# Hyena filters and DFT operands as f16 pairs, conditioning inside the first filter spectrum, row squares between the filter's steps

## The chip, the cores and the metric

One core of a Trainium2 chip runs the whole program as one launch. The metric is the device time of an execution in microseconds, as the median of several runs; lower is better.

## The reference

Two layers of a diffusion backbone: 1024 latent tokens and 256 context tokens of 1024 channels. The first layer mixes half of its channels by a 2-D Fourier transform and half by an order-2 Hyena operator, the second by neighbourhood attention; each ends with a SwiGLU. The norms are modulated by vectors that a matrix product of a conditioning vector gives (`ada_mod`). The change concerns the Hyena filters, the first norm and its modulation:

```python
def ada_mod(cond, w, b):
    m = (jax.nn.silu(cond) @ w + b)[..., None, :]
    return jnp.split(m, 6, axis=-1)

def hyena_filters(L, w1, b1, freq, w2, b2, w3):
    ...
    h = jnp.sin(freq * (z @ w1 + b1))
    h = jnp.sin(freq * (h @ w2 + b2))
    h = (h @ w3).reshape(L, 2, HY_ORDER, HY_CH)
    ...
    h = h * jnp.exp(-t01 * deltas)[:, None, None, :]
    h = h / jnp.sum(jnp.abs(h), axis=(0, 1), keepdims=True)
    fwd, bwd = h[:, 0], h[:, 1]
    return jnp.concatenate([fwd, jnp.zeros_like(fwd[:1]), bwd[:0:-1]], axis=0)

def long_conv(u, filt, skip):
    ...
    ff = jnp.fft.rfft(filt, n=2 * L, axis=0)
    y = jnp.fft.irfft(uf * ff[None], n=2 * L, axis=1)[:, :L]
    return y + u * skip
```

For each token `u = rms_norm(x, g) * (1 + scale) + shift` follows, and `p = u @ w_in` is the first large product. There are filters for length 1024 (latent, called `l`) and for length 256 (context, `c`), two orders each.

## The kernel before, in words

The program is written as Python generators that issue instructions in steps and are woven into each other in `run`. A scheduler then fixes the order of each engine's instructions before the launch; on the chip every engine issues its own in that order. Tiles come from pools with a number of buffers by tag: `p4` (`S4`, 20 of 4 KB a partition), `p2` (`S2`, 34 of 2 KB), `pt` and `pk` (`T`, `TK`), `pw` (three tags `ws`, `wh`, `wl` with two buffers each), eight PSUM banks (`ps`, `pq`). DMAs go by the SP queue (`ld`) or by the POOL queue (`ldr`, also for loads that cast).

Ahead of the input projection stand these steps.

- `filter_mlp`: two small fp32 layers with a sine behind each, for 512 latent and 128 context positions, in both directions. Its output is split for PE into a high part and a remainder, stacked on the partitions (`ta`, `tb`).
- `ada_first`: the shift and scale of the first norm. Sixteen loads `ada_k` of 512 KB, in eight steps of two, each step with four fp32 products of two columns (L423) into one PSUM bank; then four copies of its rows to SBUF (L431), sixteen small fp32 products that turn them into columns, and additions. `operand_scale` makes of them one factor, with a maximum over partitions on POOL (L1238), by which `norm_half` forms its f16 pairs.
- `filter_raw`: `w3` of the two directions is added and subtracted (L626), split into fp32r pairs (`split`: a cast on ACT, L287, and a subtraction on DVE, L289), multiplied with `ta` and `tb` and by a window (L646). For each order, 4 blocks with a forward and a backward half, even and odd.
- `filter_spectrum`: four DFT matrices (`ff`) by four blocks. For each of the sixteen pairs, an operand is formed on DVE (L707 to L713), split into an fp32r pair (L287, L289), and multiplied with the matrix, which comes as f16 high and low halves and is cast to fp32r on ACT (`cmat`, L335): three products for each of four outputs. `filter_sum` runs within: absolute values on ACT (L658, L659), a maximum and a running sum on DVE (L660, L662), a sum over partitions on PE.
- `norms` in `run`: ten row tiles of x are squared with an accumulator on ACT (L2149), a square root and reciprocal follow, then the reciprocals are spread over partitions by fp32 products of a diagonal with ones (L2158 to L2162), then 24 calls of `norm_half`, two passes on DVE and one on ACT each (L555 to L558).

In `run` before, `ada_first` is stepped from the start through `filter_raw` of the first order and drained ahead of the first spectrum. The raw values of the second order, and four `norm_half`, go into the first spectrum, the other twenty into the second. The context filter is filler work of `in_proj`, whose sixteen weight blocks follow; there its w3 sums (L626) and its operands are on POOL.

## Time and profile before

| What | Value |
|---|---|
| Runs | 2910.8, 2916.38, 2915.75 us, median 2915.75 |
| Profiled execution | 2919.95 us; its span 2918.2 us, mean TensorE clock 0.977 |
| Busy over the span | PE 2766.6, DVE 2094.0, ACT 1647.7, POOL 642.6 us |
| First product of the first spectrum | 69.67 us from the span's start |
| Last product of the second spectrum ends | about 198.2 us |
| First product of the input projection | 205.69 us |
| `ada_k` loads | 16 of 512 KB, median 6.2 us from issue to landing |
| `x_row` loads | 10 of 512 KB, median 9.8 us |

Times of a row are microseconds from the start of the span; a row of a group has its busy time, the mean of one instruction in ns, and the idle time of the engine just before. The busy time of TensorE takes in the time at a reduced clock, so the granted clock is read beside it.

### The profile page before, as it was taken

How to read it: one execution, taken by the hardware profiler on the slowest of the kernel's cores; microseconds unless marked ns; L12 is line 12 of the kernel's file. 1: busy time of each engine (PE TensorE's matmuls, PEld its weight loads, DVE VectorE, ACT ScalarE, POOL GpSimd, SP SyncE). 2: the span in 40 equal slices, each digit the busy share in tenths (PEclk: the TensorE clock that was granted, in tenths of full speed). 3: DMA queues.
4: the chain of work that ended last, by engine and by line, in shares of the span. 5: the costliest groups of instructions: out<-in, count | busy, mean ns of one | idle time of the engine just before them, and what ended most of it. 6: DMA issues, size and time to landing. Idle time of an engine off the chain costs nothing. (4 is left out here: it accounts for less than half of the span.)

```text
span 2918.2 us, 46050 instructions
## 1 busy us (share of the span) xinstructions
PE 2766.6 (95%) x16163; PEld 1714.2 (59%) x16163; DVE 2094.0 (72%) x3833; ACT 1647.7 (56%) x2899; POOL 642.6 (22%) x1057
## 2 busy tenths in 40 slices
PE   6989999999989999999999999999999999999998
PEld 3766557888879644444555844676665444444554
DVE  4778867585467798877886767776676778775765
ACT  4674324454675667654555555676664477654553
POOL 1012013354220121213120012444443022112000
PEclk8989999999999999999999999999999999999999
DMA  6574434358785555566994798777775666424753
GB/s 254 187 265 161 161 122 151 111 168 286 285 344 182 207 205 197 201 213 240 327 333 161 273 337 294 179 188 172 185 198 188 236 226 231 153 93 184 242 191 113
DMA packets 325156, 615.98 MB, mean 211 GB/s; under 512 B 90934, under 2 KB 130552, under 8 KB 324922
## 3 DMA queue, kind: packets, MB, share of 16 engines
q1 hardware_dynamic: 252378, 384.38, 39.9%
q0 software_dynamic: 70240, 224.45, 21.6%
q10 hardware_dynamic: 2304, 4.20, 0.4%
q8 instruction: 127, 2.08, 0.3%
q14 instruction: 107, 0.88, 0.1%
HBM read 455.33 MB, written 135.53 MB: 202 GB/s over the span
## 5 line engine op out<-in xcount | busy, mean ns | idle before, releaser
L1449 PE MATMUL ps<-s,s 128*128 128x512 f16 x2592 | 582.2, 382 | 14.4 <-ACT tk L1454 6.8
L1449 PEld LDWEIGHTS <-s 128*128 128x128 f16 x2640 | 259.0, 98 | 332.6 <-issue 27.8
L283 PE MATMUL ps<-s,wh 128*128 128x256 f32 (+3 forms) x1752 | 398.2, 331 | 11.1 <-ACT wh L287 5.4
L1218 ACT ACTIVATE s<-s,c 128x512 f16<-128x512 f32 (+1 forms) x324 | 233.5, 754 | 141.9 <-DMA s<-d 79.9
L1219 DVE SCALAR_TENSOR_TENSOR s<-s,c,s 128x512 f16<-128x512 f32 (+1 forms) x324 | 247.4, 794 | 84.5 <-ACT s L1218 84.1
L1666 PE MATMUL ps<-s 128*128 128x512 f16 (+2 forms) x1308 | 303.4, 378 | 2.0 <-DVE s L1219 2.0
L283 PE MATMUL pq<-s,wh 128*128 128x512 f16 (+1 forms) x1000 | 280.3, 354 | 9.8 <-DMA wh<-d 5.4
L283 PE MATMUL ps<-s,wl 128*128 128x256 f32 (+3 forms) x876 | 261.6, 331 | 1.3 <-DVE wl L289 1.2
L283 PEld LDWEIGHTS <-wh 128*128 128x128 f16 x1664 | 160.9, 99 | 170.2 <-issue 20.9
L1666 PEld LDWEIGHTS <-s 128*128 128x128 f16 x1536 | 148.5, 98 | 178.9 <-issue 6.5
L274 POOL DMA_DIRECT2D d<-s x201 | 109.0, 543 | 640.5 <-DVE s L1510 178.6
L283 PE MATMUL ps<-s,s 128*128 128x65 f16 (+5 forms) x2666 | 222.3, 236 | 27.5 <-DMA s<-s 11.4
L335 ACT CAST mat<-cs 128x1024 fp32r<-128x1024 f16 (+2 forms) x120 | 111.6, 935 | 140.6 <-PE ps L283 57.3
L283 PEld LDWEIGHTS ps<-s,wh 128*128 128x128 f32 x1088 | 177.5, 192 | 18.1 <-ACT wh L287 5.7
L283 PE MATMUL ps<-s,mat 128*128 128x512 f32 x696 | 184.7, 413 | 3.3 <-DVE s L289 2.9
L1449 PE MATMUL ps<-s,wh 128*128 128x512 f16 x616 | 184.9, 379 | 1.8 <-DVE g L1463 1.4
L283 PE MATMUL pq<-s,wl 128*128 128x512 f16 (+1 forms) x500 | 174.5, 354 | 0.5 <-DMA wl<-d 0.5
L283 PEld LDWEIGHTS <-s 128*128 128x128 f16 x2400 | 114.5, 98 | 82.9 <-DMA s<-s 11.5
L283 PEld LDWEIGHTS ps<-s,mat 128*128 128x128 f32 x696 | 136.5, 199 | 37.9 <-DVE s L289 3.8
L1251 ACT ACTIVATE t<-s 128x1024 bf16<-128x1024 f32 (+1 forms) x164 | 141.9, 867 | 12.2 <-DVE c L470 8.4
L283 PEld LDWEIGHTS ps<-s,s 128*128 128x128 f32 (+1 forms) x746 | 113.6, 192 | 32.1 <-ACT s L287 7.0
L283 PEld LDWEIGHTS <-wl 128*128 128x128 f16 x832 | 82.3, 99 | 77.4 <-issue 4.5
(431 smaller groups left out, 5477.3 us busy)
## 6 DMA issues: line engine op xcount, KB each, us to landing
s<-d SPq DMA_DIRECT2D x294, 256.0 KB, 4.0
d<-s POOLq DMA_DIRECT2D x157, 256.0 KB, 3.2
s<-in_down SPq DMA_DIRECT2D x154, 256.0 KB, 5.4
s<-in_ada_w POOLq DMA_DIRECT2D x48, 512.0 KB, 4.8
g<-in_bias POOLq DMA_DIRECT2D x128, 192.0 KB, 3.6
s<-in_gate SPq DMA_DIRECT2D x46, 512.0 KB, 3.7
s<-in_up SPq DMA_DIRECT2D x46, 512.0 KB, 4.0
d<-g POOLq DMA_DIRECT2D x87, 256.0 KB, 2.9
```

What stands on the lines that cost most here:

```text
L274: self.last_ldr = self.nc.gpsimd.dma_start(out, in_).ins
L283: self.nc.tensor.matmul(o, l, r, start=st, stop=sp)
L335: self.nc.scalar.copy(m, st)
L1218: nc.scalar.activation(hi, src, AF.Copy, scale=scale)
L1219: nc.vector.scalar_tensor_tensor(lo, src, scale, hi, op0=MUL, op1=SUB)
L1251: self.nc.scalar.activation(junk[:, :t.shape[1]], t, AF.Abs, scale=2.0 ** -15, accum_out=st[:, k:k + 1])
L1449: nc.tensor.matmul(ps, x[:, sl], y, start=first and j == 0 and x is wh and y is xh, stop=j == 3 and x is wl, skip_group_check=True)
L1666: m = nc.tensor.matmul(acc[j][:, c0:c1], x[:, sl], y[:, xs], start=first and k == 0, stop=last and k == 2, skip_group_check=True)
```

## The change

Eight edits, all in the part ahead of the input projection and in the context filter.

1. `ta`, `tb`, the pairs of w3, of the DFT operands and of the first row become f16 instead of fp32r. The matrices are used as they come, in f16, in three buffers; their cast on ACT goes.
2. The w3 of an order is divided by one factor: absolute values on ACT, sums over partitions by two bf16 products, a maximum along the row, times 2^-14.
3. The context filter loads the pairs of w3 that the latent filter has stored in DRAM instead of forming them on POOL, ACT and DVE.
4. `ada_first` is stepped in the first eight steps of the first spectrum, drained in the ninth with `operand_scale`; its loads go to `S4` buffers.
5. The squares of the rows are issued one a step between the steps of `filter_raw` and the first spectrum, no longer held behind the split of w3; three window tiles are loaded early, ahead of the rows.
6. `filter_mlp` yields twice a layer, so that the steps of w3 can come between.
7. The running sum of `filter_sum` goes from DVE to POOL.
8. In the second order, the operands of even blocks go from DVE to POOL (except those with a mask).

The constant `PAD_C` goes from 176 to 160. The core of the diff:

```diff
     def ada_first(self):
...
-            ws = [self.mat(1024, F32) for _ in range(2)]
+            ws = [self.S4() for _ in range(2)]
...
+    def split16(self, src):
+
+        t = self.S2(F16, 1024)
+        self.nc.scalar.copy(t[:, :512], src)
+        self.nc.vector.tensor_tensor(t[:, 512:], src, t[:, :512], SUB)
+        return t[:, :512], t[:, 512:]
...
     def filter_raw(self, sq, raws, os=(0, 1)):
...
+                ab = self.T(BF16, 1024)
+                ps = sums[o] = self.PS()
+                for j in (0, 1):
+                    nc.scalar.activation(ab[:, j * 512:j * 512 + 512], st[(o, j)], AF.Abs)
+                for j in (0, 1):
+                    self.mm(ps, self.ones.bitcast(BF16)[:, 1::2], ab[:, j * 512:j * 512 + 512], j == 0, j == 1)
+            yield
+            ts, big = {}, self.C(2)
+            for o in os:
+                nc.vector.tensor_reduce(big[:, 0:1], sums[o], axis=AX, op=MAX)
+                nc.vector.tensor_scalar(big[:, 1:2], big[:, 0:1], 1e-30, 2.0 ** -14, op0=MAX, op1=MUL)
+                nc.vector.reciprocal(big[:, 0:1], big[:, 1:2])
...
+                x = self.S2(F16, 1024)
+                self.half_split(t, big[:, 0:1], x[:, :512], x[:, 512:])
+                self.ldr(self.w3d[key], x)
...
     def filter_sum(self, sq, o, raw):
...
-                    nc.vector.tensor_tensor(acc, acc, t, ADD)
+                    nc.gpsimd.tensor_tensor(acc, acc, t, ADD)
...
     def filter_spectrum(self, sq, o, raw):
...
-                        (nc.vector if sq == "l" else nc.gpsimd).tensor_tensor(t, f, r, ADD if i in (0, 3) else SUB)
-                    xh, xl = self.S2(F32R), self.S2(F32R)
-                    self.split(t, xh, xl)
-                    yield xh, xl, self.cmat(2 * nb * P, a["ff_" + sq][i, b])
+                        eng = nc.vector if sq == "l" and (o == 0 or b % 2) else nc.gpsimd
+                        eng.tensor_tensor(t, f, r, ADD if i in (0, 3) else SUB)
+                    xh, xl = self.split16(t)
+                    mt = self.mat16(2 * nb * P)
+                    self.ld(mt, a["ff_" + sq][i, b])
+                    yield xh, xl, mt
...
     def run(self):
...
-        for _ in range(4):
-            next(ada1)
         with self.tc.issue_after(self.clamp), self.tc.issue_after(self.sin):
             next(fr)
-        for i, _ in enumerate(fr):
-            next(ada1, None)
-            if i in (0, 4):
-                next(ng)
-        drain(ada1)
-        self.u0col, self.usi = self.operand_scale(0, 0, (0, 1))
+        for _ in fr:
+            next(ng)
         fr = self.filter_raw("l", raws["l"], (1,))
         for i, _ in enumerate(self.filter_spectrum("l", 0, raws["l"][0])):
+            if i < 8:
+                next(ada1)
+            elif i == 8:
+                drain(ada1)
+                self.u0col, self.usi = self.operand_scale(0, 0, (0, 1))
             if i >= 2:
                 next(fr, None)
-            if i >= 11:
+            if i < 5 or i >= 11:
                 next(ng)
```

What the scheduler makes of it shows at three places. The first is ACT at the start. Before, it ran both sines of the filter's layers, the casts for the first raw products (`s_52`, `s_53` from the second sine, `s_71` from the sum of w3), and then the squares:

```order
L592 ACTIVATE s_44_142<-s_44_142 128x640
L592 ACTIVATE s_48_157<-s_48_157 128x640
L599 CAST s_52_172<-s_48_157 64x512
L601 CAST s_53_173<-s_48_157 64x512
L599 CAST s_54_178<-s_48_157 64x128
L601 CAST s_55_179<-s_48_157 64x128
L287 CAST s_71_225<-t_223 128x512
L287 CAST s_74_231<-t_229 128x512
L2149 ACTIVATE s_34_122,c_265<-s_34_122 128x1024
L2149 ACTIVATE s_35_124,c_265<-s_35_124 128x1024
```

Now five squares (the last one is shown) stand ahead of the first sine, and these rows follow:

```order
L2194 ACTIVATE s_41_136,c_240<-s_41_136 128x1024
L598 ACTIVATE s_47_148<-s_47_148 128x640
L2194 ACTIVATE s_42_138,c_240<-s_42_138 128x1024
L2194 ACTIVATE s_43_140,c_240<-s_43_140 128x1024
L2194 ACTIVATE s_44_142,c_240<-s_44_142 128x1024
L2194 ACTIVATE s_45_144,c_240<-s_45_144 128x1024
L2194 ACTIVATE s_46_146,c_240<-s_46_146 128x1024
L2196 ACT_TABLE_LOAD
L2196 ACTIVATE c_240<-c_240,c_95 128x10
L598 ACT_TABLE_LOAD
L598 ACTIVATE s_57_177<-s_57_177 128x640
L607 CAST s_61_192<-s_57_177 64x512
```

The squares, their square root and two table loads moved from behind the second sine to ahead of it. The second place is PE. Before, the last conditioning products (`mat` is a tile of `ada_k`, `c_115` the conditioning vector) were followed by the columns' products (`c_86`), the spread of the norms' reciprocals (`c_91`), and only then, eight rows on, by the first DFT product:

```order
L423 MATMUL ps_190<-mat_328,c_115 2x512 x2
L423 MATMUL ps_190<-mat_329,c_115 2x512 x2
L283 MATMUL ps_346<-c_86,g_347 128x2 x4
L283 MATMUL ps_346<-c_86,g_353 128x2 x4
L283 MATMUL ps_363<-c_86,g_364 128x2 x4
L283 MATMUL ps_363<-c_86,g_370 128x2 x4
L283 MATMUL ps_381<-t_378,c_91 128x256
L283 MATMUL ps_390<-tk_385,c_91 128x512
L283 MATMUL ps_399<-tk_394,c_91 128x512
```

Now the first conditioning products stand behind the first four DFT products (`m_117` is a matrix, `s_116` the high and low half of an operand):

```order
L283 LDWEIGHTS m_117_326
L283 MATMUL ps_331<-s_116_323,m_117_326 128x512
L427 MATMUL ps_353<-s_126_354,c_115 2x512 x2
L427 MATMUL ps_353<-s_127_355,c_115 2x512 x2
L427 MATMUL ps_353<-s_131_384,c_115 2x512 x2
L427 MATMUL ps_353<-s_132_385,c_115 2x512 x2
L427 MATMUL ps_353<-s_136_414,c_115 2x512 x2
L283 LDWEIGHTS c_206
L283 MATMUL pq_319<-s_116_323,c_206 2x512
```

The other eleven tiles of `ada_k` are spread over the rows up to the end of the third matrix. The third place is DVE in the fourth matrix of the first spectrum, where the scale of the conditioning (`c_754`) is formed. Its first row waits for POOL's maximum over partitions (L1284, formerly L1238); on POOL that stands behind the three running sums of L705. Before, the same rows stood ahead of the whole spectrum.

```order
L1285 TENSOR_SCALAR c_754<-c_754 128x1
L1286 RECIPROCAL c_754<-c_754 128x1
L689 TENSOR_TENSOR s_271_891<-ps_929,s_284_927 128x512
L1290 TENSOR_SCALAR c_754<-c_101,c_754 128x16
L1290 TENSOR_SCALAR c_754<-c_102,c_754 128x16
L559 SCALAR_TENSOR_TENSOR t_940<-s_274_898,c_754,s_176_541 128x256
L758 TENSOR_TENSOR t_944<-s_99_274 128x512
L559 SCALAR_TENSOR_TENSOR t_979<-s_274_898,c_754,s_176_541 128x256
```

An operand of that spectrum (`t_944`, L758) is now formed behind the scale and the first norm passes (L559).

More of the change, by code (lines that the diff above doesn't have):

```diff
@@ L593, in filter_mlp @@
             x = s
+            if layer == 0:
+                yield
         self.tap("mlp", x)
@@ L610, in filter_mlp @@
         self.frg, self.rn, self.kap = {}, {}, {}
+        self.w3d = {(o, eo): self.DR([P, 1024], F16) for o in (0, 1) for eo in (0, 1)}
+    def split16(self, src):
[3 more added lines that the diff above has]
+        return t[:, :512], t[:, 512:]
     def filter_raw(self, sq, raws, os=(0, 1)):
@@ L615, in filter_raw @@
         nb = 4 if sq == "l" else 1
[L616 to L629 removed]
+        w3, win = {}, {}
@@ new lines, in filter_raw @@
+        if sq == "c":
+            for key, d in self.w3d.items():
+                t = self.S2(F16, 1024)
+                self.ld(t, d)
+                w3[key] = (t[:, :512], t[:, 512:])
+        else:
+            st = {}
+            for o in os:
+                for j in (0, 1):
+                    st[(o, j)] = self.S2()
+                    self.ld(st[(o, j)], a["w3"][:, (2 * j + o) * HC:(2 * j + o + 1) * HC])
+            for b, k in ((0, 0), (0, 1), (1, 0)):
+                win[(b, k)] = self.S2()
+                self.ld(win[(b, k)], a["win_l"][b, k])
+            yield
+            sums = {}
+            for o in os:
+                ab = self.T(BF16, 1024)
+                ps = sums[o] = self.PS()
+                for j in (0, 1):
+                    nc.scalar.activation(ab[:, j * 512:j * 512 + 512], st[(o, j)], AF.Abs)
+                for j in (0, 1):
+                    self.mm(ps, self.ones.bitcast(BF16)[:, 1::2], ab[:, j * 512:j * 512 + 512], j == 0, j == 1)
+            yield
+            ts, big = {}, self.C(2)
+            for o in os:
+                nc.vector.tensor_reduce(big[:, 0:1], sums[o], axis=AX, op=MAX)
+                nc.vector.tensor_scalar(big[:, 1:2], big[:, 0:1], 1e-30, 2.0 ** -14, op0=MAX, op1=MUL)
+                nc.vector.reciprocal(big[:, 0:1], big[:, 1:2])
+                for eo, op in ((0, ADD), (1, SUB)):
+                    t = ts[(o, eo)] = self.T()
+                    nc.vector.tensor_tensor(t, st[(o, 0)], st[(o, 1)], op)
+            yield
+            for key, t in ts.items():
+                x = self.S2(F16, 1024)
+                self.half_split(t, big[:, 0:1], x[:, :512], x[:, 512:])
+                self.ldr(self.w3d[key], x)
+                w3[key] = (x[:, :512], x[:, 512:])
@@ L2146, in norms @@
             sq = self.C(10)
-            with self.follow(self.last_hi):
-                for i, t in rows:
-                    nc.scalar.activation(t, t, AF.Square, accum_out=sq[:, i:i + 1])
+            for i, t in rows:
+                nc.scalar.activation(t, t, AF.Square, accum_out=sq[:, i:i + 1])
+                yield
             nc.scalar.activation(sq, sq, AF.Sqrt, scale=1.0 / D, bias=self.eps)
```

44 lines of the change are left out of this document (21 added, 23 removed).

## The prediction

> **What bounds the kernel now.** I began with the stages (busy time by window), because the change touches only the first 206 us and, thinly, the filler work of the input projection behind them.
>
> ```profile
> 0.00:69.67 69.67, 41.06 (x143) 19.74 (x144) 28.55 (x64) 30.13 (x56) 11.19 (x27) 0.80 0.73 266
> 69.67:198.20 128.53, 118.30 (x484) 92.16 (x483) 100.28 (x161) 90.61 (x133) 1.28 (x2) 0.92 0.58 193
> 198.20:205.70 7.50, 0.17 (x2) 0.01 (x1) 0.64 (x5) 7.50 (x15) 0.00 (x0) 0.71 1.04 401
> ...
> 205.70:480.00 274.30, 263.51 (x1430) 154.76 (x1431) 210.88 (x432) 99.66 (x175) 46.61 (x53) 0.96 0.44 156
> ```
>
> The columns are window, length, busy PE, PEld, DVE, ACT, POOL, the granted TensorE clock, the DMA share and GB/s. In the first 69.67 us PE is busy 41. From 69.67 to 198.2 (the two filter spectra) it is busy 118.3 of 128.5 at a mean clock of 0.92, so 10.2 us are idle and about 8% (10.3 us) go to the slow clock. From 198.2 to 205.7 PE has nothing and ACT is full. From 205.7 on PE is the bound. Next I read what PE waited for before 206.
>
> ```profile
> PE ps L283 <- ACT s L287: 9.1, 3, 5.9
> ...
> PE ps L283 <- DVE s L289: 2.9, 2, 2.7
> ...
> PE ps L283 <- DVE s L662: 2.6, 1, 2.6
> ```
>
> The columns are the wait in all, the times, the longest. 5.9 of the first row lie before the first raw product; the other 3.2 of it, 2.9 and 2.6 are gaps inside the spectra. Then the timeline, for when the first spectrum could start and what stood ahead of it.
>
> ```profile
> 24.05 0.74 ACT L592 ACTIVATE s<-s 128x640 f32<-128x640 f32 x1 [7.56 <-DVE s L591]
> ...
> 27.42 0.79 PE L283 MATMUL ps<-s,s 128*128 128x512 f32 x1 [5.86 <-ACT s L287]
> ...
> 33.88 0.69 DVE L646 TENSOR_TENSOR s<-ps,s 128x512 f32<-128x512 f32 x1 [5.05 <-DMA s<-in_win_l]
> ...
> 44.72 1.29 DVE L713 TENSOR_TENSOR t<-s 128x512 f32<-128x512 f32 x2
> ...
> 52.37 3.08 PE L423 MATMUL ps<-mat,c 128*2 128x512 f32 x8 [2.91 <-DMA mat<-in_ada_k]
> ...
> 55.49 2.38 ACT L431 COPY g<-ps 2x512 f32<-2x512 f32 x4 [4.94 <-PE ps L423]
> ...
> 56.21 6.96 PE L283 MATMUL ps<-c,g 2*128 2x2 f32 x32 [0.77 <-ACT g L431]
> ...
> 69.67 0.84 PE L283 MATMUL ps<-s,mat 128*128 128x512 f32 x3
> ```
>
> DVE has formed the first operands by 46 (44.72 + 1.29), yet the first product with a DFT matrix (`mat`) runs at 69.67. Between them lies the conditioning: 8 MB of `ada_k` through two pairs of buffers, its products (L423), four copies on ACT (L431), the turn into columns. ACT issues in order, so the cast of the first operand stands behind copies that wait for PE. **This chain, not work, sets 69.67.**
>
> **The change, part by part.** The times are of the profiled execution, 2919.95 us with its span of 2918.2; the median of the runs is 2915.75, so 4.2 less.
>
> *A. The front without the conditioning.* The new ACT order puts five squares ahead of the first sine and five, with a square root and two table loads, between the two.
>
> ```profile
> 15.75 0.74 ACT L592 ACTIVATE s<-s 128x640 f32<-128x640 f32 x1 [4.36 <-DVE s L591]
> ...
> L2149 ACT ACTIVATE s<-s 128x1024 f32<-128x1024 f32 x10 | 10.4, 1046 | 0.0
> ...
> L2150 ACT ACT_TABLE_LOAD x1 | 1.3, 1283 | 0.0
> ...
> 35.68 3.07 DVE L646 TENSOR_TENSOR s<-ps,s 128x512 f32<-128x512 f32 x5
> ```
>
> The first sine was at 15.75; DVE now does two sums and the maximum of the w3 sums ahead of it (three 0.68 passes and three small ones), from which I subtract a little because 2 MB of `ada_k` no longer stand ahead of the w3 loads: 17.5 (bounds 15.75 and 20). The second follows at 17.5 + 0.7 + five squares at 1.04 + two table loads at 1.28 + 0.3 = 26.3; by the MLP alone it would be 24.05 - 15.75 = 8.3 after the first, 25.8. As before, 3.3 us later the first raw product: 29.6. It runs eight high halves before the first low one (at the slow clock about 0.4 each), so the first multiplication by the window is at 32.7; the window tiles are loaded ahead of the rows now, and the 5.05 wait goes. DVE then has 16 of them at 0.61 (the row with x5) and 4.3 us of others in front of the first operand: 46.5. One cast, 0.6: **47.1 instead of 69.67, 22.6 earlier** (bounds: 26, with the sine 1.75 earlier and DVE not held by the raw products; 16, with it 2.5 later and 4 lost to rows of x that land late). PE's 32 raw products fit beneath DVE here.
>
> *B. What moves into the first spectrum.*
>
> ```profile
> L423 PE MATMUL ps<-mat,c 128*2 128x512 f32 x64 | 13.4, 721 | 5.0 <-DMA mat<-in_ada_k 5.0
> ...
> L283 PE MATMUL ps<-c,g 2*128 2x2 f32 x32 | 7.0, 348 | 0.8 <-ACT g L431 0.8
> ...
> L283 PE MATMUL ps<-tk,c 128*128 128x512 f32 x4 | 3.6, 1061 | 0.0
> ...
> L283 PE MATMUL ps<-t,c 128*128 128x256 f32 x2 | 1.2, 715 | 0.0
> ...
> 50.00:60.00 10.00, 6.87 (x26) 4.01 (x27) 0.21 (x3) 4.75 (x7) 0.00 (x0) 0.56 0.28 89
> 60.00:70.00 10.00, 9.49 (x28) 6.58 (x29) 3.01 (x18) 3.19 (x7) 0.38 (x1) 0.59 0.34 100
> ```
>
> 13.4 of L423 at the mean clock 0.80-0.85 are 11.4 at full clock; 7.0 + 3.6 + 1.2 lay at 56 to 68, at a clock of 0.56 to 0.59, so 6.8. Sum 18.2, plus 0.5 for the w3 sums; bounds 15 and the measured 25.2. PE was the busy engine there, so all of it counts. Its 16 loads are issued by POOL behind two writes of w3 halves, which wait for DVE at about 31; 47 leaves time for the first six, and the later ones come in pairs between products.
>
> *C. Half precision.* The two sorts of 512-column product at full clock:
>
> ```profile
> 117.83 2.93 PE L283 MATMUL ps<-s,mat 128*128 128x512 f32 x12
> ...
> 120.59 0.62 PE L283 MATMUL pq<-s,s 128*128 128x512 f32 x2
> ...
> 187.85 1.84 PE L283 MATMUL ps<-c,s 128*128 128x1 f32 x16
> ...
> 211.82 0.27 PE L283 MATMUL pq<-s,wh 128*128 128x256 f16 x1
> 211.93 0.59 PE L283 MATMUL ps<-s,wh 128*128 128x512 f16 x2
> 212.36 0.27 PE L283 MATMUL pq<-s,wh 128*128 128x256 f16 x1
> ```
>
> Twelve fp32r in 120.59 - 117.83 = 2.76, 0.230 each; 1280 columns of f16 in 0.54, 0.216 per 512. By the code there are 384 with `mat`, 36 small ones for the first row, 32 raw ones of the second order: 452 x 0.014 = **6.3**. The lighter weights (fp32r loads take 0.19, f16 0.10) lie beneath the products.
>
> *D. Casts and waits.*
>
> ```profile
> L335 ACT CAST mat<-cs 128x1024 fp32r<-128x1024 f16 x32 | 33.4, 1051 | 34.0 <-issue 12.4 <-PE ps L283 10.4 <-PE ps L423 5.2
> ...
> L662 DVE TENSOR_TENSOR s<-s,s 128x1024 f32<-128x1024 f32 x6 | 7.3, 1211 | 0.0
> ...
> L713 POOL TENSOR_TENSOR t<-s,s 128x512 f32<-128x512 f32 x2 | 2.5, 1274 | 0.0
> ...
> 86.92 0.80 PE L283 MATMUL pq<-s,s 128*128 128x512 f32 x1 [1.98 <-ACT s L287]
> ...
> 88.03 4.81 PE L283 MATMUL ps<-s,mat 128*128 128x512 f32 x12
> ```
>
> 32 casts, 33.4 us, leave ACT, which had 90.6 of 128.5 there: this removes the 1.98 wait, and little else, since ACT ended few of PE's waits. Walking the new order by these durations I find idle PE at three places: 1.7 at the conditioning rows (four accumulator copies of 0.5 and one of 0.6 on ACT, less one conditioning product); 3.4 where the remainder of the fourth matrix's third block stands on DVE behind the scale from POOL's all-reduce and seven operations of 0.4 to 0.6; 3.3 at the start of the second spectrum (four copies and two casts, as before). That is 8.4 against 10.2. An idle time of 2 us costs more than itself: behind the one at 86.92 twelve products take 0.40 each. I keep the loss by the clock at 10.3, as fewer gaps stand against a cold start at 47.1.
>
> The Trainium skill, "TensorE: Matmul & The Clock Gate", section "What's actually happening", says that the clock halves after an idle window and returns after about 3.4 us of work. The trace has 4.8 us and more behind a gap of 2.0, so by the rule three gaps would cost about 5 and not 10.3, and the sum would be 5 lower.
>
> In the second spectrum DVE could become the bound: 32 norm passes of 512 at 0.67, 5 of 256 at 0.4, 14 remainders and 8 operands at 0.6, 4 maxima at 1.13 and small ones, 42 us by the new order, against 210 products at 0.216, 47 with the column sums (1.84 above). It fits, narrowly.
>
> *Sum.* Work after the first product: 128.5 - 10.2 - 10.3 = 108.0, less 6.3, plus 18.7, is 120.4; plus 8.4 idle and 10.3 clock: 139.1. From 47.1 the spectra end at 186.2 (before 198.2). The tail to the first projection product (table load, Silu, copies, weights' sums) keeps its 7.5: 193.7 against 205.7, **12.0 us gained**. Behind that I take nothing: the context filter loses w3 sums on POOL, 8 splits and small casts, but PE is full; bounds 0 and 5. Its one long wait is this:
>
> ```profile
> PE ps L283 <- DVE c L1316: 3.8, 1, 3.8
> ```
>
> 2919.95 - 12.0 = 2908.0 for an execution like the profiled one, and 2915.75 - 12.0 = **2903.8**, called 2904.
>
> **The rivals.** *The conditioning and PE take it all back*: either f16 products come no faster (minus 6.3), or the moved 25.2 cost their measured length (minus 6.5). Gain 5.5 to 6, or nothing with both: 2910 to 2916. Against it: the slow clock of 56 to 68.
>
> *More than forecast*: the removed casts let the operands run so far ahead that only the second spectrum's start stays idle and the clock holds (plus 5 and 5), and the projection's 3.8 wait goes: 18 to 26, 2890 to 2898. For it: ACT and DVE each lose work; against: the in-order remainders behind the conditioning scale.
>
> *Slower: POOL holds DVE.* Six 1024-wide sums and four operands go to POOL.
>
> ```profile
> 208.13 1.21 DVE L470 CUSTOM_DVE_ANT_0 t<-s,s 128x1024 bf16<-128x1024 f32 x1
> ...
> 214.39 2.28 DVE L470 CUSTOM_DVE_ANT_0 t<-s,s 128x1024 bf16<-128x1024 f32 x1
> ...
> 208.66 6.92 POOL L626 TENSOR_TENSOR t<-s,s 128x512 f32<-128x512 f32 x4 [24.87 <-DMA s<-in_w]
> ```
>
> While POOL adds (1.73 each, 1.27 elsewhere), the same DVE operation takes 2.28 and not 1.21. Ten operations, the wide ones doubled to 3.5, are 28 us of POOL; DVE loses about half of that, 14, against 7.3 + 2.7 saved. If it loses all of it, and the all-reduce stands behind three sums of 3.5, PE waits 10.5 more in the first spectrum, 2.4 by the clock, and 6 in the second: 19 lost, 7 slower, 2923. It decides from the point at which DVE's 42 us exceed PE's 47, or the all-reduce ends later than PE's arrival by more than 12.
>
> The Trainium skill, "SBUF — State Buffer", section "SBUF: two separate sides", calls the port pair of DVE and GpSimd an exclusive lock under which the loser blocks fully, for DVE operations with two SBUF inputs. The rows agree in kind (2.28 for 1.21); by full blocking this rival's 2923 holds.
>
> **How the numbers follow.** Forecast (gain 7 to 18, 2898 to 2909): 0.52. More: 0.20. Taken back: 0.17. Slower: 0.11. The range leaves out the slower case and the far end of the larger gain: 2893 to 2915. About 0.2% (5.8 us, 2909.9 and 2921.6) is what a measurement can tell from no change. Faster: 0.52 + 0.20 and a little of the third, 0.74; same 0.16; slower 0.10.
>
> **What would show it.** A: the first product with a matrix (`m`) at 43 to 52. B: the conditioning products between those of the first spectrum, with no DMA wait over 2 us. C: 0.216 between f16 products. D: three gaps as named, PE idle about 8 in the spectra. End: the first projection product near 194. I am wrong if that product comes at 194 and the whole doesn't follow, if DVE's two-input operations double for long stretches, or if the second sine waits for the rows past 30.

## The result and the profile after

The changed kernel takes 2924.92 us (median of 15 runs, 2917.42 to 2928.78) against 2913.04 for the kernel before in the same comparison: ratio 1.0031, 95% interval 1.002 to 1.0043. Two more comparisons gave 1.0023 (1.0008 to 1.0037) and 1.0025 (1.0012 to 1.0037). By these ratios it is slower by 7 to 9 us; 12 faster were forecast, and the forecast is wrong.

The windows of the changed kernel, cut where PE starts the first spectrum, the second, ends it, starts the projection, the long convolution (first L913 product), ends its inverse transform (last L1019) and starts the first feed-forward product (L1495):

```profile
0.00:50.55 50.55, 16.06 (x43) 6.24 (x43) 30.57 (x56) 22.60 (x38) 9.75 (x24) 0.96 0.94 351
50.55:140.14 89.59, 79.42 (x362) 31.02 (x362) 50.10 (x94) 35.71 (x67) 12.04 (x11) 0.91 0.44 152
140.14:198.70 58.56, 51.52 (x226) 21.70 (x226) 52.38 (x71) 35.34 (x57) 23.64 (x9) 0.94 0.62 205
198.70:207.29 8.59, 0.36 (x3) 0.01 (x1) 0.63 (x5) 8.39 (x16) 0.00 (x0) 0.80 0.95 368
207.29:455.00 247.71, 242.95 (x1354) 136.69 (x1355) 194.21 (x407) 83.51 (x147) 37.88 (x47) 0.98 0.47 163
455.00:696.50 241.50, 228.14 (x1448) 204.50 (x1446) 164.49 (x340) 121.00 (x191) 104.38 (x115) 0.97 0.55 172
696.50:983.80 287.30, 267.08 (x1747) 241.49 (x1748) 170.53 (x254) 167.41 (x274) 51.91 (x96) 0.96 0.70 260
```

The front ends 19 us earlier than in the execution shown of before (50.55 for 69.44), and all of it is gone by 207.29. Between them PE's idle time has grown; the gaps on its timeline (two shorter ones, of 0.7 to 0.8, are left out):

```profile
50.55 0.59 PE L283 MATMUL pq<-s,c 128*2 128x512 f16 x1 [7.64 <-ACT s L624]
...
128.64 0.58 PE L283 MATMUL pq<-s,m 128*128 128x512 f16 x1 [5.26 <-ACT s L624]
...
132.10 1.01 PE L283 MATMUL pq<-s,m 128*128 128x512 f16 x2 [1.60 <-DVE s L625]
...
140.14 0.38 PE L283 MATMUL pq<-s,c 128*2 128x512 f16 x1 [1.84 <-ACT s L624]
...
160.71 0.81 PE L283 MATMUL pq<-s,m 128*128 128x512 f16 x3 [2.44 <-ACT s L796]
162.68 1.23 PE L283 MATMUL ps<-s,m 128*128 128x512 f16 x3 [1.17 <-ACT s L624]
...
166.72 2.72 PE L283 MATMUL ps<-s,m 128*128 128x512 f16 x6 [2.39 <-DVE s L625]
...
179.77 0.59 PE L283 MATMUL pq<-s,m 128*128 128x512 f16 x2 [1.04 <-DVE s L625]
...
207.29 2.31 PE L283 MATMUL ps<-s,wh 128*128 128x256 f16 x6 [1.94 <-ACT wh L1264]
```

Behind 50.55 the idle time in the spectra is 17.2 (89.59 - 79.42, and 58.56 - 51.52); 8.4 was forecast. The largest gap, 5.26, hangs on the conditioning: PE waits for the cast on ACT (L624) of an operand that DVE forms behind the scale. POOL's rows and DVE's, in order of time:

```profile
98.69 2.35 POOL L705 TENSOR_TENSOR s<-s,s 128x1024 f32<-128x1024 f32 x1 [12.68 <-DVE s L703]
113.45 2.35 POOL L705 TENSOR_TENSOR s<-s,s 128x1024 f32<-128x1024 f32 x1 [12.42 <-DVE c L1278]
117.02 2.35 POOL L705 TENSOR_TENSOR s<-s,s 128x1024 f32<-128x1024 f32 x1 [1.23 <-DVE s L703]
125.17 0.38 POOL L1284 PARTITION_ALL_REDUCE c<-c  x1 [5.80 <-issue]
```

```profile
112.08 1.22 DVE L703 TENSOR_TENSOR s<-s,s 128x1024 f32<-128x1024 f32 x1
...
113.84 3.04 DVE L703 TENSOR_TENSOR s<-s,s 128x1024 f32<-128x1024 f32 x1
...
117.40 2.05 DVE L1280 SCALAR_TENSOR_TENSOR c<-c 128x1 f32<-128x1 f32 x2
...
120.58 0.14 DVE L1283 TENSOR_TENSOR c<-c 128x1 f32<-128x1 f32 x1
125.58 0.15 DVE L1285 TENSOR_SCALAR c<-c 128x1 f32<-128x1 f32 x1 [4.86 <-POOL c L1284]
```

The all-reduce has its operand at 120.72, and POOL has been free since 119.37, yet it runs at 125.17: 5.80 us of "issue", in which the profile shows nothing that POOL waits for (5.67 and 5.78 in the two other traces of this kernel). DVE stands at the row behind it (L1285) for 4.86, with the operands and remainders that PE needs queued behind. Of the all-reduce (L1284) the view by line has a row on POOL's sequencer:

```profile
L1284 POOLq MODIFY_POOL_CONFIG  x6: 8/11/37, 119.3 to 1259.3; - x6
```

It comes at 119.3, when the last sum is done. I read the 5.8 us as a change of POOL from sums to the all-reduce; the runs without those sums bear it out below. The same view of the kernel before shows such waits too:

```profile
L1238 POOLq MODIFY_POOL_CONFIG  x6: 8/37/37, 47.4 to 1255.7; - x6
L1238 POOL PARTITION_ALL_REDUCE c<-c x4: 378/380/777, 64.2 to 1479.3; - x4
...
  issue: 11.8, 2
```

Two later all-reduces waited 5.9 each on average for "issue"; the first had its change at 47.4 and its operand only at 64, so the change was hidden under the conditioning. The Trainium skill, "GPSIMD Engine Reference", section "2.1 Instruction dispatch", says that the first call of a freshly loaded kernel pays some 6 us (5.95) with no instruction to be seen for it. 5.80 agrees in size, behind a MODIFY_POOL_CONFIG row as there; what POOL does in that time no trace here shows.

**Is the execution shown of before a fair base?** A second trace of the kernel before has these windows:

```profile
0.00:65.74 65.74, 39.08 (x142) 19.23 (x142) 28.54 (x63) 29.88 (x56) 11.19 (x27) 0.84 0.76 281
65.74:134.61 68.87, 62.26 (x258) 48.55 (x258) 51.15 (x86) 43.85 (x64) 0.00 (x0) 0.93 0.52 174
134.61:192.17 57.56, 53.16 (x226) 40.78 (x227) 49.45 (x77) 47.27 (x70) 1.28 (x2) 0.97 0.68 224
192.17:199.85 7.68, 0.17 (x3) 0.01 (x1) 0.63 (x5) 7.68 (x15) 0.00 (x0) 0.85 1.01 358
...
696.80:974.10 277.30, 263.43 (x1747) 239.72 (x1746) 170.69 (x253) 167.15 (x274) 52.12 (x96) 0.97 0.73 268
```

Its first projection product is at 199.85, not 205.69; a third execution with that front (below) has 200.63. The one I forecast from had a late front. Three traces of the changed kernel have 207.29, 210.30 and 209.94. By means (202.1 and 209.2) the change **loses 7.1 us by the first projection product**, and not the 1.6 that the two first traces show.

The lengths of the two spectra vary far less than where they start. From the first product of each to the first of the next, and to the end of the last one (198.90 in the first trace of the changed kernel, so 58.76 and not the 58.56 of the window above):

| Kernel | First spectrum | Second spectrum |
|---|---|---|
| before, three traces | 71.30, 68.87, 70.69 | 57.43, 57.56, 59.02 |
| changed, three traces | 89.59, 89.98, 90.01 | 58.76, 58.74, 58.73 |
| changed, POOL's part undone (e3, e12) | 85.12, 83.85 | 55.95, 56.44 |
| changed, first three sums on DVE (e6) | 83.86 | 60.12 |
| conditioning in front, POOL's part kept (e4) | 64.95 | 59.43 |
| conditioning in front, POOL's part undone (e5) | 65.71 | 56.06 |

Within the changed kernel, idle time and slow clock trade places: its other two traces have gaps of 2.86 and 2.96 where the first has 5.26, and 12.1 and 14.8 idle in all for 17.2, at a mean clock of 0.88 for 0.91 in the first spectrum. The length is the same, so I go by the lengths.

### The profile page after: what moved, and what is told of

Read it like the earlier page. It is cut to its first block, busy times and chain, and to the rows that moved or that the text cites. A ratio compares the mean times of both kernels' runs of the same rounds, so it can differ in the third digit from the quotient of the medians.

```text
span 2918.1 us, 46007 instructions
## 1 busy us (share of the span) xinstructions
PE 2751.5 (94%) x16167; PEld 1656.0 (57%) x16167; DVE 2091.8 (72%) x3824; ACT 1614.8 (55%) x2860; POOL 667.3 (23%) x1068
## 5 line engine op out<-in xcount | busy, mean ns | idle before, releaser
L1495 PE MATMUL ps<-s,s 128*128 128x512 f16 x2592 | 579.9, 381 | 15.2 <-ACT tk L1500 6.8
L1495 PEld LDWEIGHTS <-s 128*128 128x128 f16 x2640 | 257.9, 98 | 332.0 <-issue 25.6
L283 PE MATMUL ps<-s,wh 128*128 128x256 f32 (+3 forms) x1848 | 405.5, 328 | 12.0 <-ACT wh L287 8.7
L283 PE MATMUL ps<-s,wl 128*128 128x256 f32 (+3 forms) x924 | 268.5, 328 | 2.9 <-DVE wl L289 2.9
L283 PE MATMUL pq<-s,wh 128*128 128x512 f16 (+1 forms) x904 | 255.6, 364 | 9.0 <-DVE s L2001 7.2
L1712 PEld LDWEIGHTS <-s 128*128 128x128 f16 x1536 | 148.3, 98 | 179.1 <-issue 6.5
L1495 PE MATMUL ps<-s,wh 128*128 128x512 f16 x616 | 185.1, 379 | 1.2 <-DVE g L1509 1.2
L283 PEld LDWEIGHTS <-s 128*128 128x128 f16 x2500 | 124.1, 98 | 104.7 <-issue 17.4
L283 PE MATMUL pq<-s,wl 128*128 128x512 f16 (+1 forms) x452 | 160.6, 363 | 0.0
L1264 ACT ACTIVATE s<-t,c 128x512 f16<-128x512 f32 x174 | 116.1, 712 | 34.4 <-DVE c L1363 15.0
L339 ACT CAST mat<-cs 128x1024 fp32r<-128x1024 f16 (+2 forms) x80 | 74.7, 941 | 92.0 <-PE ps L283 36.2
L1265 DVE SCALAR_TENSOR_TENSOR s<-t,c,s 128x512 f16<-128x512 f32 x174 | 124.8, 747 | 1.0 <-ACT s L1264 1.0
L1495 PE MATMUL ps<-s,wl 128*128 128x512 f16 x308 | 116.7, 379 | 0.0
```

The source lines that it names most:

```text
L283: self.nc.tensor.matmul(o, l, r, start=st, stop=sp)
L339: self.nc.scalar.copy(m, st)
L1264: nc.scalar.activation(hi, src, AF.Copy, scale=scale)
L1265: nc.vector.scalar_tensor_tensor(lo, src, scale, hi, op0=MUL, op1=SUB)
L1495: nc.tensor.matmul(ps, x[:, sl], y, start=first and j == 0 and x is wh and y is xh, stop=j == 3 and x is wl, skip_group_check=True)
L1712: m = nc.tensor.matmul(acc[j][:, c0:c1], x[:, sl], y[:, xs], start=first and k == 0, stop=last and k == 2, skip_group_check=True)
```

## The experiments

First projection product is meant wherever a time stands without more; the landmark varies by up to 3 us between executions of the changed front, by up to 6 of the front before. Each run below has one trace. The later sums (e10 and f4) are one kernel in two comparisons, with ratios 0.9997 and 1.0014, so a difference of 0.0017 between two comparisons says little. All runs:

| Run | First projection product | Ratio to before, 95% interval |
|---|---|---|
| changed kernel, three comparisons | 207.29, 210.30, 209.94 | 1.0031; 1.0023; 1.0025 |
| before against itself (c_before) | 199.85 | 0.9997 (0.9984 to 1.001) |
| e1_old_turn | 207.15 | 1.0024 (1.0005 to 1.0044) |
| e2_new_turn | 200.63 | 1.0003 (0.9987 to 1.0019) |
| e3_sums_dve | 200.37 | 0.9978 (0.996 to 0.9996) |
| e4_cond_front | 197.85 | 0.9973 (0.9955 to 0.9992) |
| e5_half_only | 196.47 | 0.9952 (0.9934 to 0.9969) |
| e6_first_sums_dve | 203.85 | 0.9986 (0.9974 to 0.9997) |
| e7_turn_behind | 208.63 | 0.9994 (0.998 to 1.0008) |
| e8_squares_late | 213.97 | 0.9998 (0.9985 to 1.0011) |
| e10_sums_later | 208.97 | 0.9997 (0.9985 to 1.001) |
| e12_late_dve | 204.47 | 0.998 (0.9966 to 0.9994) |
| f1_work_turn | 207.41 | 1.0016 (1.0003 to 1.0028) |
| f2_bank_turn | 209.95 | 1.0031 (1.0018 to 1.0044) |
| f4_later_again | 209.11 | 1.0014 (0.9999 to 1.0029) |

### The conditioning and POOL: four corners

POOL's part undone, conditioning left inside:

```
-    nc.gpsimd.tensor_tensor(acc, acc, t, ADD)
+    nc.vector.tensor_tensor(acc, acc, t, ADD)
...
-    eng = nc.vector if sq == "l" and (o == 0 or b % 2) else nc.gpsimd
+    eng = nc.vector if sq == "l" else nc.gpsimd
```

> The changed kernel with the six 1024-wide sums and the four operands back on DVE. Theory 1, POOL beside DVE is the dear part: the second spectrum falls from 58.6 to 52 to 55, the wait of 5.3 at 123 falls below 2, the first projection product comes at 197 to 202, and 5 to 8 of it reach the end if nothing behind swallows it: 2917 to 2920. Rival (DVE is the bound by its own work, 52.4 of 58.6 busy, and gets 10 more): the second spectrum stays at 57 to 60, 2923 to 2927. Theory 3: first projection product earlier, the end unchanged.

200.37. The gap of 5.26 is gone, and the all-reduce starts 0.14 after its operand:

```profile
120.66 0.15 DVE L1283 TENSOR_TENSOR c<-c 128x1 f32<-128x1 f32 x1
121.36 0.15 DVE L1285 TENSOR_SCALAR c<-c 128x1 f32<-128x1 f32 x1 [0.55 <-POOL c L1284]
```

The operand comes when it did before (120.66 and 120.58); only what POOL had in front of it is gone. The windows of the two spectra:

```profile
50.52:135.64 85.12, 80.57 (x362) 31.42 (x362) 49.33 (x98) 35.73 (x67) 3.57 (x7) 0.91 0.48 162
135.64:191.59 55.95, 51.12 (x226) 21.62 (x226) 50.01 (x78) 35.86 (x58) 1.28 (x2) 0.97 0.65 213
```

The second takes 55.95 and not 58.76, though DVE has more operations there (78 for 71): DVE's own work is not the bound, and the projection comes where theory 1 has it. The spectrum is 1 above the range given, and the total, 2909.04, is 8 to 11 below it. With POOL's part undone the change is faster than the kernel before (0.9978).

The conditioning back in front, POOL's part kept:

```
-    ws = [self.S4() for _ in range(2)]
+    ws = [self.mat(1024, F32) for _ in range(2)]
...
     drain(mlp)
+    for _ in range(4):
+        next(ada1)
...
     for _ in fr:
+        next(ada1, None)
         next(ng)
+    drain(ada1)
+    self.u0col, self.usi = self.operand_scale(0, 0, (0, 1))
...
-    if i < 8:
-        next(ada1)
-    elif i == 8:
-        drain(ada1)
-        self.u0col, self.usi = self.operand_scale(0, 0, (0, 1))
```

> The changed kernel with the conditioning back in front of the first spectrum (its loads in the mat buffers, its products between the raw products, the scale ahead of the spectrum), half precision and POOL's work kept. Theory 1: the first product with a matrix at 66 to 71 again, the spectra shorter by the moved 14 and by the 5.3 gap, so the first projection product at 204 to 209: the move gained nothing net, 2922 to 2927. Rival (the move was worth what its 18.6 in front say, less 14): first projection product at 211 to 215, 2928 to 2932. If half precision and POOL were worth what I forecast without the move (6.3 and 4), 197 to 200.

```profile
64.87:129.82 64.95, 61.73 (x267) 26.39 (x267) 46.50 (x80) 32.62 (x61) 11.18 (x6) 0.94 0.52 175
129.82:189.25 59.43, 54.37 (x226) 22.31 (x226) 53.26 (x73) 35.30 (x56) 31.58 (x9) 0.91 0.60 198
```

197.85, at the place that I had given half precision and POOL without the move. The first spectrum starts at 64.87 and takes 64.95; PE's idle time in both is 8.3. With POOL's part kept the move loses some 11 us net (209.2 less 197.85), where I had it gain 3.9 (22.6 less 18.7).

Both edits at once. Of the change the half-precision pairs remain, and with them the factor of w3, the context filter's loads of stored pairs, the new place of the squares and the steps of the MLP:

> The changed kernel with both the conditioning back in front and POOL's sums and operands back on DVE: of the change the half-precision pairs remain, with their loads and the two steps of the MLP. Theory 1a (the moved conditioning costs about 9 net and POOL beside DVE about 7, and they add): first projection product at 189 to 193. Theory 1b (POOL is harmful only through the conditioning chain that waits behind it, as with the conditioning in front the second spectrum has time): 196 to 199, as with the conditioning alone in front (197.85). Rival (DVE then has 10 us more and is the bound): 200 to 204. End: 2908 to 2914, or 2902 to 2908 with 1a.

```profile
65.44:131.15 65.71, 63.17 (x267) 26.93 (x267) 48.60 (x86) 32.51 (x61) 1.29 (x2) 0.92 0.51 169
131.15:187.22 56.07, 51.42 (x226) 21.60 (x226) 49.92 (x78) 35.63 (x57) 1.07 (x2) 0.97 0.65 214
```

196.47: theory 1b, by the projection. With the conditioning in front, POOL's part costs 1.4 there, which is within the spread, and 2.6 by the lengths of the spectra. The total, 2904.23 us, lies where theory 1a had it, and is faster than both kernels: 0.9952.

The three sums of the first spectrum on DVE, the rest on POOL:

```
-    nc.gpsimd.tensor_tensor(acc, acc, t, ADD)
+    (nc.gpsimd if o else nc.vector).tensor_tensor(acc, acc, t, ADD)
```

> The changed kernel with the three 1024-wide sums of the first spectrum back on DVE, those of the second and the operands still on POOL. If the all-reduce's wait behind POOL's sums is the dear part: the wait of 5.3 at 123 falls to about 2, as with all sums on DVE (1.99), and the first projection product comes at 203 to 205. If it is the second spectrum, where DVE is slowed while POOL adds: the second spectrum stays at 57 to 60 and the first projection product at 205 to 207.5. End: 2918 to 2925 in either case.

203.85, as expected if the all-reduce's wait is the dear part; it follows its operand without a wait. The first spectrum takes 83.86 and not 89.6 to 90.0: the three sums ahead of the all-reduce cost some 5 to 6 us. The second stays long, 60.12, for 56.0 and 56.4 with everything on DVE and 58.7 in the changed kernel: POOL costs some 3 there. The total, 2914.74, is 3 below the range given.

The four corners, by the projection: 196.5 (conditioning in front, sums on DVE), 197.9 (in front, POOL), 200.4 (inside, DVE), 209.2 (inside, POOL). Each move alone costs 1 to 4 us, both together 13; but three of the corners are single traces of a landmark that varies by 3 to 6. The lengths of the two spectra together say it more firmly: POOL's part adds 2.6 with the conditioning in front (124.4 for 121.8) and 7.3 to 8.5 with it inside (148.3 to 148.7 for 141.1 and 140.3). In the first spectrum alone it adds nothing in front (64.95 for 65.71) and 4.5 to 6.2 inside.

### The front

```
-    nc.scalar.activation(t, t, AF.Square, accum_out=sq[:, i:i + 1])
+    with self.tc.issue_after(self.sin):
+        nc.scalar.activation(t, t, AF.Square, accum_out=sq[:, i:i + 1])
```

> The changed kernel with the ten squares over the rows of x held back until the second sine of the filter MLP has issued, so that the first sine waits for no row and the square root's table loads leave the gap between the sines. Theory for the front (rows that land late and table loads between the sines cost 3 to 5): second sine at 23 to 26 and not 28.4, first product with a matrix at 46 to 49 and not 51.1 to 52.6, first projection product at 202 to 206. Rival (the front is bound by DVE's multiplications): first product with a matrix within 1 of 51. By this edit the scheduler also puts the ACT operations of the output projection in the order of the kernel before. Theory 4: the stretch from 697 falls from 286 to 287 to 276 to 281, total 2909 to 2915. If that order has no part in it: 285 to 288, total 2917 to 2923.

The changed kernel's ACT, then this run's:

```profile
13.05 1.06 ACT L2194 ACTIVATE s<-s 128x1024 f32<-128x1024 f32 x1 [2.55 <-DMA s<-in_x_row]
...
19.10 0.72 ACT L598 ACTIVATE s<-s 128x640 f32<-128x640 f32 x1
...
25.45 1.28 ACT L2196 ACT_TABLE_LOAD   x1
...
28.36 0.74 ACT L598 ACTIVATE s<-s 128x640 f32<-128x640 f32 x1
```

```profile
26.41 0.74 ACT L598 ACTIVATE s<-s 128x640 f32<-128x640 f32 x1 [7.49 <-DVE s L597]
27.05 1.04 ACT L2195 ACTIVATE s<-s 128x1024 f32<-128x1024 f32 x1
...
34.32 0.60 ACT L607 CAST s<-s 64x512 f16<-64x512 f32 x1
```

The second sine is 2 earlier. But seven squares of 1.04 now stand between it and the casts that PE needs, the first product with a matrix is at 56.4 and the projection at 213.97: the expectation failed, and it doesn't tell what the rows cost in the place that the change gives them. The stretch from 697 (below) takes 281.3 and the total is 2917.87, so neither of the two cases given for it came whole. With POOL's part undone as well:

> The changed kernel with the squares held back as in the run before and POOL's sums and operands back on DVE; half precision and the moved conditioning stay. If the parts add (front 4 earlier, POOL 7 earlier): first projection product at 195 to 198, as with half precision alone (196.5), total 2902 to 2908. If the second spectrum is bound by DVE and takes back what the front gains: 199 to 202, total 2906 to 2912.

204.47, behind both ranges given, and 4.1 behind the same without the late squares: the 5 lost in front stay lost. The spectra are about as long as in e3.

### Behind the projection: counters and order

The windows of 696 to 984 (from the last L1019 to the first L1495 product; "the stretch" in what follows) show a second loss: 287.30 against 277.30 and 278.2 of before (286.0 in the mean of three traces of the changed kernel). The helpers `T` and `PS` (L242, L251) choose a buffer pool and a PSUM bank by counters; the change alters the number of calls in the spectra, and with it every later choice. Setting the counters at load of the conditioning for the other layers and behind the projection, once to the old values in the changed kernel, once to the new ones in the kernel before:

```
     drain(ng)
+    self.tk, self.pk = 3, 5
     self.load_cond()
...
     for _ in filt:
         pass
+    self.tk, self.pk = 5, 6
```

> The changed kernel with one edit: the two counters that choose the work buffer (T: pt or pk) and the PSUM bank (PS) are set, behind the spectra and behind the input projection, to the values that they had there before the change. Theory 1 (the loss is in the two spectra: conditioning chain and POOL beside DVE): no difference from the changed kernel, 2922 to 2927, first projection product still near 207.3. Theory 2 (the shifted turn of the buffers costs time behind the spectra, where the traces lose 9 us between 700 and 981): 2912 to 2917, 8 to 12 less than the changed kernel, with the first 207 us unchanged. Theory 3 (a stretch behind 700 bound by DMA swallows what arrives earlier): no difference, as theory 1.

> The kernel before with nothing of the change but the shift of the two counters, set at the same two places to the values that they have in the changed kernel. Theory 1 and theory 3: 2911 to 2915, as the kernel before. Theory 2: 2920 to 2925, 8 to 12 more than before, all of it behind 480.

1.0024 and 1.0003: set back at both places, the counters change neither total. They do move time: in the first of the two the stretch falls to 280.4, but the projection ahead of it takes 254.0 and not 248 to 250. The order on ACT differs too, since the scheduler places instructions by modelled times. The changed kernel, then before, ACT in the output projection:

```profile
821.98 1.06 ACT L1297 ACTIVATE t<-s 128x1024 bf16<-128x1024 f32 x1 [5.76 <-DMA s<-in_wk]
...
823.55 1.04 ACT L287 CAST wh<-ws 128x1024 fp32r<-128x1024 f32 x1
```

```profile
821.08 0.63 ACT L496 ACTIVATE tk<-s 128x512 f32<-128x512 f32 x1 [0.97 <-DVE s L1197]
821.62 1.04 ACT L1251 ACTIVATE t<-s 128x1024 bf16<-128x1024 f32 x1
...
824.68 1.05 ACT L287 CAST wh<-ws 128x1024 fp32r<-128x1024 f32 x1 [1.93 <-DMA ws<-in_w_out]
```

A sum over absolute values, scheduled one place earlier, waits 5.76 for its load, and a square and a weight cast stand behind it; in before a square stands ahead of it, and it waits for nothing; there the cast waits 1.93 for its own load. Two edits tell order and buffers apart: the old counters behind the projection only, which leaves that order, and each sum two tiles later, which puts it behind the third cast and its square:

```
+held = []
...
-    self.abs_sums([t], self.qs[:, k:k + 1])
+    held.append((t, k))
+    if len(held) > 2:
+        s, i = held.pop(0)
+        self.abs_sums([s], self.qs[:, i:i + 1])
...
         yield
+    for s, i in held:
+        self.abs_sums([s], self.qs[:, i:i + 1])
```

> The changed kernel with the counters set to their old values behind the input projection only. Its order on ACT in the output projection is word for word that of the changed kernel: the first sum over absolute values stands ahead of a square and a weight cast. Theory 2 (buffers and banks by themselves): the stretch between the landmarks near 697 and 984 falls from 286 to 287 to about 278, total 2914 to 2919. Theory 4 (the order on ACT there, whatever the buffers): the stretch stays at 284 to 289, total 2921 to 2927.

> The changed kernel with one edit in the scan of the later weights: each sum over absolute values is emitted two tiles after its load, not with it. The first 620 us are those of the changed kernel (first projection product at 207 to 210). On ACT the first sum now stands behind the third weight cast and its square. Theory 4 (a sum that waits 5.8 for its load holds the casts behind it): the stretch from 697 is 276 to 281 and not 286 to 287, total 2914 to 2918. Rival (the stretch is set by the DMA engines, full there, not by the order): 285 to 288, total 2922 to 2927.

The stretch is 285.1 with the order kept and 282.8 with the sums later, where a sum still waits 3.19 for its load ahead of a cast; the totals, 2916.54 and 2918.06, stand beside no run of the changed kernel on the same chip. One agrees with theory 4 by the stretch and not by the total, so both follow once more beside the changed kernel, the first with its two counters apart.

```
     for _ in filt:
         pass
+    self.tk = 5
```

> The changed kernel with only the work-buffer counter set back behind the input projection, the order on ACT unchanged. Theory 2 (buffers): 6 to 9 below the changed kernel of this call if the work buffers are the cause, the stretch from 697 at 277 to 281. Theory 4 (order on ACT): within 3 of it, the stretch at 284 to 288.

```
     for _ in filt:
         pass
+    self.pk = 6
```

> The changed kernel with only the PSUM counter set back behind the input projection, the order on ACT unchanged. Theory 2 (banks): 6 to 9 below the changed kernel of this call if the banks are the cause. Theory 4: within 3 of it, the stretch at 284 to 288.

> The changed kernel with each sum over absolute values emitted two tiles after its load, now beside the changed kernel in one call. Theory 4: 4 to 9 below it, the stretch at 277 to 283. Theory 2: within 3 of it.

The controls, the two kernels as they are:

> The changed kernel as it is, a second look with its own trace. All theories: 2920 to 2926, 1.002 to 1.0045 of the kernel before. What it tells apart is whether the loss that the first trace shows between 700 and 984 (287.3 against 278.2) belongs to the kernel: if so it comes again at 285 to 289; if it is one execution's, it comes at 278 to 283.

> The kernel before as it is, against itself: ratio 0.998 to 1.002. Its second trace shows how far landmarks behind 460 move between two executions of one kernel; I expect the first 206 us within 0.5 and the stretch from 700 to 984 within 4.

> The changed kernel as it is, on the chip of the three others of this call: 2922 to 2927 by all theories, the yardstick for them.

The kernel before, against itself, had the projection 5.8 earlier, where I expected 0.5 at most. Beside 2922.66 for the changed kernel stand 2921.09, 2924.73 and 2919.86; the stretch is 284.8, 284.6, 285.2 and 280.5. In all six traces with the first order it is 284.6 to 287.3, in both with the sums later 280.5 and 282.8: 2 to 7 us less. But that the order is the cause isn't shown. In e4 and e5 no sum waits there, as in the kernel before, and the stretch takes 284.8 and 284.6 all the same; the weight cast behind the first sum waits 5.40 and 4.41 for its own load of `w_out`. Other edits have 278.5 to 283.9, each with an order of its own, and the totals (1.0014 against 1.0025, intervals that overlap) don't resolve it. When these loads come, and why, wasn't tried; the DMA engines are busy 0.70 of the stretch in the changed kernel and 0.73 in before. The cause of this second loss stays open.

## Why the prediction was wrong

**A, the front: mis-sized on both sides.** Forecast 47.1 instead of 69.67, 22.6 gained. The first product with a matrix came at 51.07, 52.62 and 52.07, and the front of before has 69.67, 65.98 and 63.96: by means 14.6. New front: I put the first sine at 17.5, the second at 26.3, the first raw product at 29.6; they came at 19.10, 28.36 and 31.82. The chain was right, its size wrong: I charged the first sine nothing for five squares ahead of it on ACT, which wait for rows of x (DVE had its input ready at 17.4). Of the 4.0 that the first matrix product is late, 2.2 are there at the first raw product; the other 1.8 come behind it. Old front: one execution was taken as the rule, at the late end of three; why it varies stays open.

**B, the moved work: right.** 18.7 forecast. PE's rows of it in the first spectrum are 13.0 of L427, 3.7 of the turn into columns, 2.3 of the norms' spread and 0.8 of the w3 sums: 19.8, some at the slow clock. (The 19.4 by which the first spectrum grows between the corners without POOL is near by chance: the spread stands inside in both, and 2.0 of it are idle time.) No conditioning product waited for a load.

**C, half precision: right by its rows.**

```profile
90.89 2.75 PE L283 MATMUL ps<-s,m 128*128 128x512 f16 x12
93.48 1.03 PE L283 MATMUL pq<-s,s 128*128 128x512 f16 x4
```

Twelve in 93.48 - 90.89 = 2.59, 0.216 each. Of the 36 small products of the first row, which I gave the same gain, the twenty with the column tile `c` went the other way: fifteen of them take 0.30 to 0.31 until the next product starts, for 0.23 before, some 1.2 in all. What remains in e5 takes 11.6 us off the median (2904.23 against 2915.83), 5.6 by the first projection product; how much of that is half precision and how much the squares, the casts or the context filter, no run separates.

**D, casts and waits: the step that failed.** I forecast 8.4 idle and 10.3 by the clock, 18.7. The first trace has 17.2 idle, and 0.09 of 79.42 and 0.06 of 51.52 are 10.2 by the clock; the two others have 12.1 and 16.4, and 14.8 and 13.0. That is 27 to 29 in all three, some 9 more than forecast, and that the clock's 10.2 met the forecast in one of them was luck. With POOL's part undone it is 9.4 + 8.8 in e3 and 9.5 + 8.6 in e12, 18.2 in both: without POOL the step would have held as a sum. What failed is that the sum gave POOL's part no price. In the first spectrum the sentence that put 3.4 at "the remainder of the fourth matrix's third block" let the all-reduce start when its operand was there; it started 4.5 us later, behind the sums and POOL's change, and the gaps there sum to 6.9, 5.1 and 5.1 in the three traces, for 1.4 to 3.5 in the three runs without those sums. In the second, which I had called fitting "narrowly", there are gaps of 2.44, 1.17, 2.39 and 1.04; 3.5 to 4.8 us of idle time remain there without POOL's part too (e3, e12, e5), which I had not put there either, and the shorter gap at its start (1.84 for 3.3) makes up for part of it. I had this mechanism as the slower rival, at 0.11, with a price of 19: its sign was right, its price 7 to 9, and it ran through the all-reduce for another reason than I wrote. The sums there took 2.35 and not 3.5; it was the 5.8 of the change to the all-reduce that no other work covered any more.

In the second spectrum POOL and DVE hold each other up, both ways:

```profile
160.39 2.74 POOL L705 TENSOR_TENSOR s<-s,s 128x1024 f32<-128x1024 f32 x1 [1.22 <-issue]
165.62 13.55 POOL L705 TENSOR_TENSOR s<-s,s 128x1024 f32<-128x1024 f32 x2 [2.49 <-DVE s L703]
```

```profile
160.84 2.84 DVE L758 TENSOR_TENSOR tk<-s 128x512 f32<-128x512 f32 x1
...
177.48 3.91 DVE L625 TENSOR_TENSOR s<-t,s 128x512 f16<-128x512 f32 x2 [0.53 <-ACT s L624]
```

A DVE pass of 0.68 takes 2.84 while POOL's sum runs, and ends 0.55 behind it (163.68 and 163.13). Two POOL sums take 13.55 while DVE is full, 6.8 each, about twice the 3.5 that I had priced. By the prediction's page of the Trainium skill, "SBUF — State Buffer", section "SBUF: two separate sides", the loser blocks fully; the rows agree.

**The tail:** 8.59 for 7.5; by the last product's end 8.4, 9.5 and 9.7 in the three traces for 7.5, 7.7 and 7.2 before. It is 9.3 in e5 too, so neither POOL nor the moved conditioning makes it; the cause is open. **Behind it, "I take nothing":** wrong twice, with opposite signs. To the first L913 product the changed kernel takes 247.7, 249.8 and 249.5, before 254.0 and 254.9: 5.4 gained by the means, at the end of the bounds given. That the context filter's lost splits and casts are the cause isn't shown: in e1, which has them too and only sets the counters back, it takes 254.0. Then the output projection's stretch loses 8, from a cause that stays open. That PE is full there was no reason for zero.

The sum: at the first projection product 12.0 gained was forecast, and 1.6 lost by the two first traces. Front 4.0 late (51.07 for 47.1), spectra 8.5 longer (147.6 from 51.07 to 198.70, for 139.1), tail 1.1: the 13.6 between 193.7 and 207.29. By the means of three traces on each side the miss is 19.1 (12.0 gained, 7.1 lost): 8.0 in the front, 9.4 in the spectra, 1.7 in the tail.

## What to carry to other kernels

Price an edit's parts together as well as apart: POOL's part cost 2.6 us of the spectra while the conditioning stood in front, and 7 to 8 once its all-reduce stood inside, behind the sums. Before a short operation is moved, look at what it has in front of it on its own engine now: here 5.9 us of change-over stood as "issue" before two of four all-reduces in the profile of before, and only the place of the first had hidden it. And take the base from more than one execution: this front varied by 5.7 us, half of the gain forecast, while the first spectrum's length stayed within 0.5 in three traces of the changed kernel.

## What was not expected of the hardware

POOL took 5.8 us to go from an elementwise sum to the all-reduce over partitions, with no busy instruction shown (119.37 to 125.17; 11.8 for two in the kernel before), and started it 0.14 us after its operand in e3, where MODIFY_POOL_CONFIG stands at 87.0. Even two DVE operations of one column (L1280) took 2.05 beside a POOL sum, and 0.23 in the run without it (e3).
